# The u projection as a stage of its own behind q, k and v, read back from DRAM 512 tokens at a time

## The chip, the core and the metric

One NeuronCore of a Trainium2 chip runs the whole kernel in one launch. The metric is the device time of that launch in microseconds (us). Its engines are called PE (TensorE, the matrix unit), DVE (VectorE), ACT (ScalarE), POOL (GpSimd) and SP (SyncE, which issues most DMAs here); each works through its own instructions in order.

## The reference

One encoder block: 16 meta tokens ahead of 2048 tokens, 1024 wide, float32. Attention has 4 query heads and 2 key/value heads of 128; the second half of the block, u, is 512 wide and is mixed by a two-dimensional Fourier transform over tokens and over each group's 128 channels.

```python
hn = rms_norm(h, g_mix)
proj = hn @ w_in                      # q 512, k 256, v 256, u 512
q = axial_rope(rms_norm(q, g_q)); k = axial_rope(rms_norm(k, g_k))
attn = softmax(q @ k.T / sqrt(128)) @ v
f = fft2(u as 4 groups of 128, axes=(tokens, channel), norm="ortho").real
four = f @ w_fourier                  # by group
mixed = concat(rms_norm(attn, g_attn_out), rms_norm(four, g_fourier_out))
h = h + mixed @ w_out
h = h + relu(rms_norm(h, g_mlp) @ w_up)**2 @ w_down
return rms_norm(h, g_final)[:, 16:]
```

## The kernel before

A float32 operand is split into a high and a low part (cast by ACT, remainder by DVE's L71), and a product is three matmuls: high x high, low x high, high x low (mm3, lines L80, L81, L82; L83 to L85 in the changed file). Where the text says "split", it means this. Both halves of a split are needed before the low matmuls can run.

The stages follow one another in the program, and within most of them two generators are interleaved by hand:

- *Chunks j = 0 to 7 of 256 tokens.* `prep` loads x (`load_x`, on SP), normalizes it, transposes it on PE (pt) and splits it into hth and htl. `proj_qkv` multiplies by the weights of q (tile pq) and of k and v (pkv), 512 columns at a time, for two halves of 128 tokens. `proj_u` multiplies the same parts by the weights of u, 256 tokens at a time, and adds the result (pu) into two resident tiles, UA and EV, which hold sums and differences of mirrored tokens. `post` norms and rotates q and k, splits q, k, v, transposes (ptq, ptk) and stores them to DRAM (q_d, k_d, v_d); it is a generator that `side()` advances between the projections. The meta rows' k and v (pkv_m, t = 16) come behind chunk 7.
- *Folds.* `fold` and `fold_even` (lines L506 to L517) halve UA and EV once more on DVE and ACT. They stand in chunk 7, between `proj_u` and `proj_qkv`.
- *Fourier.* `fourier`: channel products pa from EV and UA (with rem, a few rows put together on DVE), split into ahi and alo; then products py with table tiles thi, tlo, 258 columns wide; results go back into EV, UA through DVE.
- *Attention*, generator `attention`, in 16 units. A unit has 18 steps and lags 2 steps over the next (UNIT = 20). A step makes two score tiles (s, three matmuls each), copies them to S on ACT, and keeps running maxima M on DVE. When M is complete, PE transposes it (pm_m), and the maxima mb come from that. Then DVE subtracts mb from S, ACT takes the exponential, DVE adds to acc, splits the weights into ph and pl, and PE multiplies them by v (o). S_BUFS = 8 tiles of scores are kept. Units 0 and 1 (`NATIVE = 2`) don't split: PE multiplies the float32 S by vn directly (L842).
- *out_f* (pof: the Fourier half through w_fourier and w_out), then *poa* and the *MLP* (pup, pdn) and last block-wise products (ux, uy, dx, dy).

`att.upto(n)` runs attention up to step n; `mix(gen, n, a0, a1)` spreads steps a0 to a1 over the n yields of another stage. Before, Fourier takes steps 0 to 30 (FLEAD), out_f most of 30 to 84, its last five yields (HELD) 84 to 88, the MLP the rest. The pools give the buffers, the framework the waits; each engine's order is the program's with little moved.

Of the kernel before, what the change touches and what calls it, by code (L numbers as in the profile page):

```python
# [40 lines left out]
NATIVE = 2  # L41
# [6 lines left out]
FLEAD = 30  # L48
SKIP = 5
# [86 lines left out]
def encoder_block(ctx: ExitStack, tc: tile.TileContext, x, meta, w_in, w_f,  # L136
# [18 lines left out]
    mid = Lines(tc.alloc_tile_pool(name="mid", bufs=1), small)  # L155
    edge = ctx.enter_context(tc.tile_pool(name="edge", bufs=1, side="right"))
# [3 lines left out]
    wu = Lines(tc.alloc_tile_pool(name="wu", bufs=1, side="right"), small)  # L160
# [39 lines left out]
    h_d = [dram.tile([P, D], F32, name=f"h_d{t}") for t in range(NT)]  # L200
    m_d = dram.tile([P, KT, 512], F32, name="m_d")
# [72 lines left out]
    def prep(j):  # L274
# [10 lines left out]
        for kk in range(KT // 2):  # L285
# [27 lines left out]

    def spread_m():

        shape = [P, 2, MR // META, META]
        hT["m"] = []
        for kq in range(KT // 4):
            tiles = [t2k(f"ht{e}_m_{kq}", [P, 4, MR]) for e in "hl"]
            for i in range(2):  # L320
                for t, src, eng in zip(tiles, hT[LAST][2 * kq + i], (nc.scalar.copy, nc.vector.tensor_copy)):
                    eng(t[:, 2 * i:2 * i + 2].rearrange("p k (r n) -> p k r n", n=META),
                        bc(f32v(src[:, :, 256:]).rearrange("p k (r n) -> p k r n", r=1), shape))
            hT["m"].append(tiles)
# [5 lines left out]

    def proj_u(j):
        n = 256 + META if j == LAST else 256
        n0 = META + 256 * j
        for cp in range(0, NG, 2):
            if j == LAST:
                pss = [bank(f"pu_{j}_{cp + c}", (P, 1, n)) for c in range(2)]
            else:
                pss = [(tbank if j == 0 and cp == 0 else bank)(f"pu_{j}_{cp}", (P, 2, n))]
            for c in range(2):
                cc = 1024 + (cp + c) * P  # L340
                o = pss[c][:, 0] if j == LAST else pss[0][:, c]
# [47 lines left out]
    def post(j, a, pq, pkv):  # L389
# [14 lines left out]
        with ExitStack() as behind:  # L404
            for i in first_acts if m else ():
                behind.enter_context(tc.issue_after(i))
            for h in range(h0, 6):
                nc.scalar.activation(t1[:rows, h], src(h), AF.Square, accum_out=ss[:rows, h:h + 1])
# [30 lines left out]
        for _ in range(4 if j == 0 else 1):  # L439
            yield  # L440
# [61 lines left out]
    def fold(src, g):  # L502

        t = tp.tile([P, D], F32, name=f"fold{g}", tag="x", bufs=3)[:, :QUART]
        low, high = src[:, g, 0:QUART], src[:, g, QUART + 1:HALF + 1][:, ::-1]
        nc.vector.tensor_tensor(t, low, high, op=ALU.add)  # L506
        nc.vector.tensor_tensor(high, low, high, op=ALU.subtract)
        nc.scalar.copy(low, t)
# [1279 lines left out]
```

## Time and profile before

| | |
|---|---|
| median of 3 runs (lowest, highest) | 2293.54 us (2292.48, 2294.43) |
| span of the profiled execution | 2291.4 us |
| PE busy | 2278.1 us, 99% |
| DVE busy | 1718.7 us, 75% |
| ACT busy | 1280.6 us, 56% |
| POOL busy | 184.0 us, 8% |
| DMA | 307.23 MB, mean 134 GB/s |

The profiled execution's own time is its span. Matmuls overlap in PE's pipeline, so a PE that is shown busy is not necessarily at its peak: a 512-wide matmul is recorded with 0.39 us, while the next starts 0.23 us behind it.

Rough places in the trace: chunks up to 304 us, the meta rows' pkv_m to 309.4, pa from 309.9, py 315.0 to 417.3, scores from 327.2, pof from 424.5, poa from 587.5, pup from 623.1, ux from 1674.2.

### The profile page before, as it was taken

Reading aid. Unit: us, or ns where it says so; the run is one execution under the profiler, and the core shown is the slowest. Engines: PE = TensorE matmul, PEld = TensorE weight load, DVE = VectorE, ACT = ScalarE, POOL = GpSimd, SP = SyncE. Lnnn points to the kernel's source line nnn. Section 1 sums busy time; section 2 is a strip of 40 time slices with the busy share of each in tenths; the row PEclk is TensorE's granted clock in tenths of the full one; section 3 lists DMA queues with packets and bytes.
Section 4 is the critical chain, followed back from the end, with each engine's and each line's share of the span. In section 5 each row is a group of like instructions: output and inputs, shape, how many; then the busy total and the mean of one; then the engine's idle time right before and its main releaser. Section 6 shows DMA issues by size and latency. Waiting matters only on the chain.

```text
span 2291.4 us, 30005 instructions
## 1 busy us (share of the span) xinstructions
PE 2278.1 (99%) x10846; PEld 1883.0 (82%) x10846; DVE 1718.7 (75%) x2448; ACT 1280.6 (56%) x2303; POOL 184.0 (8%) x235
## 2 busy tenths in 40 slices
PE   9999999999999999999999999999999999999998
PEld 7888988777888888888888888888888888888887
DVE  6435588999986877986887877885875656697796
ACT  6443356566665655665765775664665545543344
POOL 2212120222000000000000100000000000200000
PEclk9999999999999999999999999999999999999999
DMA  6343252543533222333342453224454444865442
GB/s 213 100 119 102 78 169 79 190 137 120 166 117 108 96 87 79 114 114 106 97 157 87 157 175 104 92 82 170 140 177 158 152 152 156 303 193 165 129 138 83
DMA packets 178069, 307.23 MB, mean 134 GB/s; under 512 B 14960, under 2 KB 63728, under 8 KB 177536
## 3 DMA queue, kind: packets, MB, share of 16 engines
q1 hardware_dynamic: 159136, 262.89, 34.9%
q0 software_dynamic: 18640, 42.16, 6.2%
q8 instruction: 85, 1.39, 0.3%
q14 instruction: 64, 0.52, 0.1%
q10 hardware_dynamic: 144, 0.26, 0.0%
HBM read 225.27 MB, written 79.99 MB: 133 GB/s over the span
## 4 chain that ended last, share of the span: by engine, by line
PE 94%; DVE 3%; DMA 1%; ACT 1%; issue 1%; POOL 0%; SPq 0%; POOLq 0%; DVEq 0%; ACTq 0%
PE pdn L80 5%; PE pdn L82 5%; PE pdn L81 5%; PE pup L80 5%; PE pup L82 5%; PE pup L81 5%; PE s L80 3%; PE s L82 3%; PE s L81 3%; PE ux L80 2%; PE ux L81 2%; PE ux L82 2%; PE dx L80 2%; PE dx L82 2%; PE dx L81 2%; PE o L81 2%
## 5 line engine op out<-in xcount | busy, mean ns | idle before, releaser
L80 PE MATMUL pdn<-wh_dn,ah 128*128 128x512 f32 x512 | 201.5, 394 | 0.2 <-ACT r L1154 0.2
L80 PE MATMUL pup<-mTh,wh_up 128*128 128x512 f32 x512 | 201.5, 394 | 0.0
L81 PE MATMUL pup<-mTl,wh_up 128*128 128x512 f32 x512 | 200.7, 392 | 0.0
L82 PE MATMUL pup<-mTh,wl_up 128*128 128x512 f32 x512 | 200.4, 391 | 0.0
L81 PE MATMUL pdn<-wl_dn,ah 128*128 128x512 f32 x512 | 199.9, 390 | 0.0
L82 PE MATMUL pdn<-wh_dn,al 128*128 128x512 f32 x512 | 198.7, 391 | 0.0
L773 ACT COPY S<-s 128x512 f32<-128x512 f32 x256 | 148.4, 584 | 55.6 <-PE s L82 48.5
L70 ACT CAST wh_up<-wr_up 128x512 fp32r<-128x512 f32 x128 | 79.4, 620 | 164.3 <-PE pup L81 76.5
L832 DVE TENSOR_TENSOR S<-S,mb 128x1024 f32<-128x1024 f32 x128 | 154.8, 1218 | 8.4 <-ACT mb L803 8.2
L71 DVE TENSOR_TENSOR pl<-S,ph 128x512 fp32r<-128x512 f32 x196 | 132.3, 696 | 11.0 <-ACT ph L70 10.7
L833 ACT ACTIVATE S<-S 128x1024 f32<-128x1024 f32 x114 | 120.7, 1060 | 34.7 <-DVE S L832 34.1
L70 ACT CAST wh_dn<-wr_dn 128x512 fp32r<-128x512 f32 x128 | 79.1, 620 | 107.9 <-PE pdn L82 52.6
L71 DVE TENSOR_TENSOR wl_up<-wr_up,wh_up 128x512 fp32r<-128x512 f32 x128 | 87.6, 687 | 68.1 <-ACT wh_up L70 63.3
L839 DVE TENSOR_TENSOR acc<-acc,S 128x1024 f32<-128x1024 f32 x110 | 134.1, 1219 | 1.3 <-ACT S L833 1.1
L71 DVE TENSOR_TENSOR wl_dn<-wr_dn,wh_dn 128x512 fp32r<-128x512 f32 x128 | 87.2, 687 | 60.2 <-ACT wh_dn L70 51.8
L70 ACT CAST ph<-S 128x512 fp32r<-128x512 f32 x196 | 118.7, 620 | 15.9 <-PE o L82 12.5
L70 ACT CAST ah<-a 128x1024 fp32r<-128x1024 f32 x56 | 58.5, 1048 | 118.2 <-issue 60.8
L779 DVE TENSOR_TENSOR M<-M,S 128x1024 f32<-128x1024 f32 x96 | 118.0, 1229 | 6.7 <-ACT S L773 6.0
L80 PEld LDWEIGHTS pdn<-wh_dn,ah 128*128 128x128 f32 x512 | 96.1, 188 | 23.5 <-ACT r L1154 3.6
L80 PE MATMUL s<-q,kt 128*128 128x512 f32 (+1 forms) x272 | 113.0, 415 | 0.1
L82 PEld LDWEIGHTS pdn<-wh_dn,al 128*128 128x128 f32 x512 | 96.2, 188 | 19.9
L82 PEld LDWEIGHTS pup<-mTh,wl_up 128*128 128x128 f32 x512 | 96.2, 188 | 19.4
(345 smaller groups left out, 6413.0 us busy)
## 6 DMA issues: line engine op xcount, KB each, us to landing
wr_up<-in_w_up_dram SPq DMA_DIRECT2D x128, 256.0 KB, 2.8
wr_dn<-in_w_down_dram SPq DMA_DIRECT2D x128, 256.0 KB, 2.6
a<-s_d SPq DMA_DIRECT2D x42, 512.0 KB, 3.6
R<-in_w_up_dram SPq DMA_DIRECT2D x16, 1024.0 KB, 5.2
s_d<-s SPq DMA_DIRECT2D x64, 256.0 KB, 2.2
d<-in_w_down_dram SPq DMA_DIRECT2D x26, 512.0 KB, 5.0
s_d<-c SPq DMA_DIRECT2D x48, 256.0 KB, 2.4
x<-in_x_dram SPq DMA_DIRECT2D x16, 512.0 KB, 4.9
```

The lines of the kernel that those rows point to most:

```text
L70: self.high = nc.scalar.copy(hi, src)
L71: self.low = nc.vector.tensor_tensor(lo, src, f32v(hi), op=ALU.subtract)
L80: nc.tensor.matmul(out, a[0], b[0], start=first, stop=False, skip_group_check=chain)
L81: nc.tensor.matmul(out, a[0], b[1], start=False, stop=False, skip_group_check=chain)
L82: nc.tensor.matmul(out, a[1], b[0], start=False, stop=last, skip_group_check=chain)
L773: nc.scalar.copy(S[:, i % 2], ps)
L779: nc.vector.tensor_tensor(M, M, S, op=ALU.max)
L832: nc.vector.tensor_tensor(S, S, mb, op=ALU.subtract)
L833: nc.scalar.activation(p, S, AF.Exp, scale=ISQ)
L839: nc.vector.tensor_tensor(acc, acc, p, op=ALU.add)
```

## The change

- `proj_u` goes. In each chunk, `prep` also stores hth and htl to u_d in DRAM (64 stores of 256 KB on SP's queue). u_d has four blocks of 512 tokens.
- The weights of u are loaded and split in chunks 2 to 5 (two k per chunk), instead of at the start.
- Behind pkv_m comes `u_stage`: four parts of four result tiles each (pu_0 to pu_3), 8 values of k per part, matmuls 512 tokens wide. Parts 0 and 1 each cover one block of tokens and all 4 groups of channels; parts 2 and 3 each cover two blocks and two groups. It reads u_d back, 512 KB per load (hu), one load per k in parts 0 and 1 and two in parts 2 and 3, into 6 buffers (HG_BUFS), and yields after each k. The folds of parts 2 and 3 are queued as `todo`: one per yield while there are matmuls, and the rest in yields of their own behind the last matmul.
- The 16 meta tokens' u has matmuls of its own (`u_meta`: pum, pumt); before they rode on chunk 7's matmuls, which were 272 wide for that.
- The first 4 yields of u_stage (U_FIRST) come before attention starts; the others take attention steps 0 to 62 (ULEAD). Fourier then takes 62 to 84, out_f 84 to 104 (ALEAD = 20), the step to the MLP 4 more; the MLP starts at 108 instead of 88.
- `NATIVE = 0`: units 0 and 1 are split like the others.
- Unit 0's scores use the same two PSUM buffers as the others' instead of alternating with a free bank.

```diff
-NATIVE = 2
+NATIVE = 0
 LAG = 2
 WAKE = 6
 UNIT = 18 + LAG
 TURNS = 3
 LEAD = 4
 AHEAD = 30
-FLEAD = 30
-SKIP = 5
+ULEAD = 62
+FLEAD = 84
+U_FIRST = 4
+ALEAD = 20
+HG_BUFS = 6
...
+            for e, t in enumerate((hi, lo)):
+                nc.sync.dma_start(u_d[j // 2][:, 2 * kk:2 * kk + 2, e, j % 2 * 256:j % 2 * 256 + 256], f32v(t))
...
-    def proj_u(j):
...
-            for _ in proj_u(0):
-                side()
...
-                for src in (EV, UA):
-                    for g in range(NG):
-                        fold(src, g)
-                    for g in range(0, NG, 2):
-                        fold_even(src, g)
-                wu.release()
-                ft = Lines(tc.alloc_tile_pool(name="ft", bufs=1, reuse_waits="tile"), small)
-                load_tables(0)
+            if 2 <= j < 6:
+                for k in (2 * j - 4, 2 * j - 3):
+                    load_w(k, 1024)
+                    split_w(k, 1024)
...
+    def u_stage():
+
+        todo = []
+        for n, part in enumerate(([(0, g) for g in range(NG)], [(1, g) for g in range(NG)],
+                                  [(b, g) for b in (2, 3) for g in (0, 1)], [(b, g) for b in (2, 3) for g in (2, 3)])):
+            ps = {bg: bank(f"pu_{n}_{i}") for i, bg in enumerate(part)}
+            for k in range(KT):
+                h = {}
+                for b in sorted({b for b, _ in part}):
+                    h[b] = hg.tile([P, 2, 512], R32, name=f"hu_{n}_{b}_{k}", tag="hu", bufs=HG_BUFS)
+                    nc.sync.dma_start(f32v(h[b]), u_d[b][:, k])
+                for b, g in part:
+                    mm3(nc, ps[b, g], w_op(k, 1024 + g * P, 1024 + (g + 1) * P), (h[b][:, 0], h[b][:, 1]),
+                        k == 0, k == KT - 1, True)
+                    if k == KT - 1:
+                        n0 = META + 512 * b
+                        y = ps[b, g]
+                        if b < 2:
+                            nc.scalar.copy(UA[:, g, n0:n0 + 512], y)
+                        else:
+                            r = slice(L - n0 - 511, L - n0 + 1)
+                            y = y[:, ::-1]
+                            nc.vector.tensor_tensor(EV[:, g, r], UA[:, g, r], y, op=ALU.add)
+                            nc.vector.tensor_tensor(UA[:, g, r], UA[:, g, r], y, op=ALU.subtract)
+                if todo:
+                    f, *of = todo.pop(0)
+                    f(*of)
+                yield
+            if n == 1:
+                nc.vector.tensor_tensor(EV[:, :, 1025:1032], UA[:, :, 1025:1032], UA[:, :, 1033:1040][:, :, ::-1], op=ALU.add)
+                nc.vector.tensor_tensor(UA[:, :, 1025:1032], UA[:, :, 1025:1032], UA[:, :, 1033:1040][:, :, ::-1],
+                                        op=ALU.subtract)
+                nc.vector.tensor_copy(EV[:, :, 1032:1033], UA[:, :, 1032:1033])
+            if n > 1:
+                g = part[0][1]
+                todo += [(fold, src, i) for src in (EV, UA) for i in (g, g + 1)]
+                todo += [(fold_even, src, g) for src in (EV, UA)]
+        for f, *of in todo:
+            f(*of)
+            yield
+
+    us = u_stage()
+    for i in range(U_FIRST):
+        side()
+        if i == 1:
+            u_meta()
+        next(us)
+    drain(*pend)
...
-            if u == 0 and i % 2:
-                ps = bank("s_" + nm)
-            else:
-                ps = app.tile([P, 512], F32, name="s_" + nm, tag="S", bufs=2)
+            ps = app.tile([P, 512], F32, name="s_" + nm, tag="S", bufs=2)
...
+    mix(us, 38 - U_FIRST, 0, ULEAD)
+    hg.release()
+    wu.release()
+    ft = Lines(tc.alloc_tile_pool(name="ft", bufs=1, reuse_waits="tile"), small)
+    load_tables(0)
+    fp = Lines(tc.alloc_tile_pool(name="fp", bufs=1, reuse_waits="tile"), small)
+    four = fourier()
...
-    mix(with_weights(four, 9), 19, 0, FLEAD, SKIP - 1)
+    mix(with_weights(four, 10), 20, ULEAD, FLEAD)
...
-    mix(itertools.islice(of, 34 - HELD), 34 - HELD, FLEAD, need[0])
-    mix(of, HELD, need[0], need[0] + LEAD)
+    mix(itertools.islice(of, 34 - HELD), 34 - HELD, FLEAD, need[0] + ALEAD)
+    mix(of, HELD, need[0] + ALEAD, need[0] + ALEAD + LEAD)
```

How each engine's order changes at three places. The names are those of the text above with the numbers of chunk, unit, part or buffer behind them.

**DVE, the folds.** Before, in chunk 7, as pu of the last groups comes in:

```order
L362 TENSOR_TENSOR EV_70<-UA_69,pu_7_2_3000 128x256
L363 TENSOR_TENSOR UA_69<-UA_69,pu_7_2_3000 128x256
L506 TENSOR_TENSOR fold2_3078<-EV_70 128x516
L507 TENSOR_TENSOR EV_70<-EV_70 128x516
L357 COPY UA_69<-pu_7_3_3001 128x16
L358 COPY EV_70<-pu_7_3_3001 128x1
L533 MEMSET rem0_3122 128x384
L362 TENSOR_TENSOR EV_70<-UA_69,pu_7_3_3001 128x256
```

At that place PE goes on with chunk 7's pq and pkv, 96 matmuls of 512 columns behind the last one of pu_7_3:

```order
L82 MATMUL pu_7_3_3001<-hth_7_3_2843,wl512_7_326 128x272
L80 MATMUL pq_7_0_3147<-wh1024_0_212,hth_7_0_2641 128x512
L81 MATMUL pq_7_0_3147<-wl1024_0_213,hth_7_0_2641 128x512
L82 MATMUL pq_7_0_3147<-wh1024_0_212,htl_7_0_2642 128x512
L80 MATMUL pq_7_0_3147<-wh1024_1_218,hth_7_0_2641 128x512
L81 MATMUL pq_7_0_3147<-wl1024_1_219,hth_7_0_2641 128x512
```

Now DVE has, behind the last pu of part 3 (EV and UA <- pu), the same folds among the softmax of units 2 and 3:

```order
L74 TENSOR_TENSOR pl_2_7_0_3983<-S_2_6_3497,ph_2_7_0_3982 128x512
L74 TENSOR_TENSOR pl_2_7_1_3990<-S_2_6_3497,ph_2_7_1_3989 128x512
L787 TENSOR_TENSOR M_3_3947<-M_3_3947,S_3_4_3979 128x1024
L471 TENSOR_TENSOR fold2_4002<-EV_70 128x516
L471 TENSOR_TENSOR fold3_4014<-EV_70 128x516
L472 TENSOR_TENSOR EV_70<-EV_70 128x516 x2
L847 TENSOR_TENSOR acc_2_3835<-acc_2_3835,S_2_8_3558 128x1024
L74 TENSOR_TENSOR pl_2_9_0_4020<-S_2_8_3558,ph_2_9_0_4019 128x512
L74 TENSOR_TENSOR pl_2_9_1_4027<-S_2_8_3558,ph_2_9_1_4026 128x512
L787 TENSOR_TENSOR M_3_3947<-M_3_3947,S_3_6_4012 128x1024
L840 TENSOR_TENSOR S_2_10_3611<-S_2_10_3611,mb_2_3788 128x1024
L471 TENSOR_TENSOR fold2_4047<-UA_69 128x516
```

The folds moved from beside the projections of chunk 7 to between steps of M, acc and pl of attention.

**PE, behind the last matmul of u.** Now, from the last pu_3_3 to the first pa:

```order
L85 MATMUL pu_3_3_3637<-hu_3_3_7_3951,wl512_7_1663 128x512
L83 MATMUL s_3_4_3975<-q_3_3839,kt_0_1_1_3326 128x512
L84 MATMUL s_3_4_3975<-q_3_3839,kt_0_1_1_3326 128x512
L85 MATMUL s_3_4_3975<-q_3_3839,kt_0_1_1_3326 128x512
L83 MATMUL o_2_3836<-ph_2_7_0_3982,vt_0_1_1_3334 128x512
L83 MATMUL s_3_5_3996<-q_3_3839,kt_0_1_1_3326 128x512
L84 MATMUL s_3_5_3996<-q_3_3839,kt_0_1_1_3326 128x512
L85 MATMUL s_3_5_3996<-q_3_3839,kt_0_1_1_3326 128x512
L83 MATMUL s_3_6_4008<-q_3_3839,kt_0_1_1_3326 128x512
L84 MATMUL s_3_6_4008<-q_3_3839,kt_0_1_1_3326 128x512
L85 MATMUL s_3_6_4008<-q_3_3839,kt_0_1_1_3326 128x512
L535 MATMUL pa0_0_4207<-cw0_298,EV_70 128x128
```

Where pq and pkv followed the last u before, there are now scores of unit 3 and value products of unit 2, and then pa, the first Fourier products.

**SP, chunk 0.** Before, behind the fourth pair of weights (wraw0 and wraw512 are the q, k, v weights of one k):

```order
L226 DMA wraw512_3_155<-in_w_in_dram 128x512
L483 DMA gqk_140<-g_rows 128x512
L170 DMA x_1_0_277<-in_x_dram 128x1024
L170 DMA x_1_1_279<-in_x_dram 128x1024
L226 DMA wraw0_4_236<-in_w_in_dram 128x512
```

Now, from the last of the eight stores of chunk 0's parts:

```order
L300 DMA u_d0_130<-htl_0_3_220 128x2x256
L230 DMA wraw0_4_249<-in_w_in_dram 128x512
L230 DMA wraw512_4_251<-in_w_in_dram 128x512
L230 DMA wraw0_5_259<-in_w_in_dram 128x512
L230 DMA wraw512_5_261<-in_w_in_dram 128x512
L230 DMA wraw0_6_269<-in_w_in_dram 128x512
L230 DMA wraw512_6_271<-in_w_in_dram 128x512
L230 DMA wraw0_7_279<-in_w_in_dram 128x512
L230 DMA wraw512_7_281<-in_w_in_dram 128x512
L451 DMA gqk_144<-g_rows 128x512
L173 DMA x_1_0_290<-in_x_dram 128x1024
L173 DMA x_1_1_292<-in_x_dram 128x1024
```

x_1, the tokens of chunk 1, moved behind eight stores of u_d and the weights of k = 4 to 7.

More of the change, by code (lines that the diff above doesn't have):

```diff
@@ L155, in encoder_block @@
     mid = Lines(tc.alloc_tile_pool(name="mid", bufs=1), small)
+    wu = Lines(tc.alloc_tile_pool(name="wu", bufs=1), small)
     edge = ctx.enter_context(tc.tile_pool(name="edge", bufs=1, side="right"))
@@ L200, in encoder_block @@
     h_d = [dram.tile([P, D], F32, name=f"h_d{t}") for t in range(NT)]
+    u_d = [dram.tile([P, KT, 2, 512], F32, name=f"u_d{b}") for b in range(4)]
     m_d = dram.tile([P, KT, 512], F32, name="m_d")
@@ L319, in spread_m @@
             tiles = [t2k(f"ht{e}_m_{kq}", [P, 4, MR]) for e in "hl"]
[L320 to L323, printed above, removed]
+            for e, (t, eng) in enumerate(zip(tiles, (nc.scalar.copy, nc.vector.tensor_copy))):
+                eng(t.rearrange("p k (r n) -> p k r n", n=META),
+                    bc(f32v(hm[:, 4 * kq:4 * kq + 4, e]).rearrange("p k (r n) -> p k r n", r=1), shape))
             hT["m"].append(tiles)
@@ L403, in post @@
         src = lambda h: pq[:rows, h * P:(h + 1) * P] if h < 4 else pkv[:rows, (h - 4) * P:(h - 3) * P]
[L404 to L408, printed above, removed]
+        for h in range(h0, 6):
+            nc.scalar.activation(t1[:rows, h], src(h), AF.Square, accum_out=ss[:rows, h:h + 1])
         rs = rstd_of(tp, ss[:rows, h0:], 6 - h0, HD, f"h{h0}", rows)
@@ L632, in encoder_block @@
                     a += 1
-            if j != LAST:
-                for _ in proj_u(j):
-                    side()
         for _ in nxt:
@@ L641, in encoder_block, with u_meta @@
     wqk.release()
-    fp = Lines(tc.alloc_tile_pool(name="fp", bufs=1, reuse_waits="tile"), small)
+    hg = Lines(tc.alloc_tile_pool(name="hg", bufs=1, reuse_waits="tile"), small)
+    def u_meta():
+        ps = bank("pum")
+        for k in range(KT):
+            nc.tensor.matmul(ps[:2 * META], hm[:, k].rearrange("p l n -> p (l n)"), W[k, 512][0], start=k == 0, stop=False,
+                             skip_group_check=True)
+            nc.tensor.matmul(ps[:META], hm[:, k, 0], W[k, 512][1], start=False, stop=k == KT - 1, skip_group_check=True)
+        um = hg.tile([P, 512], F32, name="um")
+        nc.scalar.copy(um[:2 * META], ps[:2 * META])
+        both = hg.tile([P, 64], F32, name="both")
+        nc.vector.tensor_tensor(both[:2 * META, :META], ident[:2 * META, :META], ident[:2 * META, META:2 * META], op=ALU.add)
+        pt = bank("pumt", (P, NG, META))
+        for g in range(NG):
+            nc.tensor.matmul(pt[:, g], um[:2 * META, g * P:(g + 1) * P], both[:2 * META, :META], start=True, stop=True)
+        nc.vector.tensor_copy(UA[:, :, 0:META], pt)
+        nc.vector.tensor_copy(EV[:, :, 0:1], pt[:, :, 0:1])
@@ new lines, in u_stage @@
+    def u_stage():
[3 more added lines that the diff above has]
+            ps = {bg: bank(f"pu_{n}_{i}") for i, bg in enumerate(part)}
+            for k in range(KT):
+                h = {}
[30 more added lines that the diff above has]
+            f(*of)
+            yield
@@ L684, in fourier @@
                 yield
-    four = fourier()
-    next(four)
-    drain(*pend)
-    trp.release()
-    tp.release()
     app = tc.alloc_tile_pool(name="app", bufs=1, space=PSUM)
@@ L896, in attention @@
             yield
-    HELD = 5
+    HELD = 0
     wt = {}
@@ L1239, in encoder_block @@
     n0, n1 = 8 + 2 + 8 * 15 + 8, 8 + 8 * 13 + 8 + 4
-    a0, a2 = need[0] + LEAD, need[3] + 1
+    a0, a2 = need[0] + ALEAD + LEAD, need[3] + 1
     a1 = a0 + (a2 - a0) * n0 // (n0 + n1)
```

80 lines of the change are left out of this document (19 added, 61 removed).

## The prediction

> **What bounds the kernel now.** I read the page first, then a table of stages cut at the starts of pm_m, then PE's waits, and last single instructions for prices. In the page's first part the figures are busy time, share of the span and instructions. In the second each digit is a fortieth of the span.
>
> ```profile
> span 2291.4 us, 30005 instructions
> PE 2278.1 (99%) x10846; PEld 1883.0 (82%) x10846; DVE 1718.7 (75%) x2448; ACT 1280.6 (56%) x2303; POOL 184.0 (8%) x235
> PEclk9999999999999999999999999999999999999999
> GB/s 213 100 119 102 78 169 79 190 137 120 166 117 108 96 87 79 114 114 106 97 157 87 157 175 104 92 82 170 140 177 158 152 152 156 303 193 165 129 138 83
> PE 94%; DVE 3%; DMA 1%; ACT 1%; issue 1%; POOL 0%; SPq 0%; POOLq 0%; DVEq 0%; ACTq 0%
> ```
>
> TensorE is the bound and its clock is full throughout: what the change takes from PE's work is worth its full time, and every us for which PE stands still is lost. But the average hides one region. VectorE stands at 75% over the span, but not evenly.
>
> The next table gives each stretch, its length, then busy time by engine. It is cut where PE computes the row maxima of attention units 0 to 5 (pm_m; each waits for the unit's last M on DVE).
>
> ```profile
> 342.80:394.40 51.60, 51.60 (x308) 41.57 (x309) 46.50 (x65) 33.49 (x57) 3.57 (x5) 1.00 0.29 78
> 394.40:450.50 56.10, 55.45 (x274) 42.02 (x271) 53.94 (x78) 32.19 (x58) 15.93 (x19) 1.00 0.53 169
> 450.50:510.30 59.80, 58.82 (x267) 46.80 (x267) 57.60 (x82) 37.55 (x75) 13.60 (x17) 1.00 0.41 143
> 510.30:568.40 58.10, 58.02 (x261) 45.50 (x260) 56.05 (x77) 36.06 (x67) 13.06 (x19) 1.00 0.37 123
> 568.40:653.90 85.50, 85.50 (x405) 70.20 (x406) 69.65 (x106) 52.85 (x95) 7.54 (x8) 1.00 0.47 149
> 653.90:741.30 87.40, 87.40 (x393) 71.86 (x392) 69.40 (x93) 53.51 (x88) 4.13 (x6) 1.00 0.39 118
> ```
>
> In the second to fourth stretch DVE is busy 96% of the time, beside a PE that is at its limit too: both engines carry the same load there. From the fifth on DVE has slack. So the question to the change is not only what PE saves, but where it leaves DVE's work without PE work beside it.
>
> **Prices.** A busy PE row overlaps the next one, so prices are steps from start to start.
>
> ```profile
> 73.97 0.28 PE L81 MATMUL pu<-htl,wh 128*128 128x256 f32 x1
> 76.61 0.28 PE L82 MATMUL pu<-hth,wl 128*128 128x256 f32 x1
> ...
> 76.95 0.60 PE L291 MATMUL pt<-ident,x 128*128 128x128 f32 x4
> 77.30 0.36 PE L80 MATMUL pu<-hth,wh 128*128 128x256 f32 x1
> ...
> 100.06 0.39 PE L80 MATMUL pq<-wh,hth 128*128 128x512 f32 x1
> 103.24 0.39 PE L82 MATMUL pq<-wh,htl 128*128 128x512 f32 x1
> ...
> 369.63 1.88 PE L842 MATMUL o<-S,vn 128*128 128x512 f32 x4
> 370.94 0.79 PE L80 MATMUL s<-q,kt 128*128 128x512 f32 x1
> 371.58 0.40 PE L81 MATMUL s<-q,kt 128*128 128x512 f32 x1
> ```
>
> 73.97 to 76.61 are 22 steps of 256 columns: 0.120 us. Four of 128 columns take 0.35 (76.95 to 77.30), so I put the small ones (pa, pm, pd) at 0.1. 100.06 to 103.24 are 14 steps of 512: 0.227. From 369.63 to 371.58 run four records of the unsplit value product and one split one: (1.95 - 0.23) / 4 = 0.43 each.
>
> ```profile
> L80 PE MATMUL pu<-hth,wh x256: 277/283/365, 33.0 to 281.0; 128*128 128x256 f32 x112, 128*128 128x272 f32 x16
> L842 PE MATMUL o<-S,vn x64: 590/592/697, 347.9 to 440.5; 128*128 128x512 f32 x64
> ...
> 519.35 0.69 DVE L71 TENSOR_TENSOR ohl<-O,ohl 128x512 fp32r<-128x512 f32 x1
> 519.96 0.42 DVE L71 TENSOR_TENSOR yl<-UA,yh 128x256 fp32r<-128x256 f32 x1
> 520.29 1.22 DVE L839 TENSOR_TENSOR acc<-acc,S 128x1024 f32<-128x1024 f32 x1
> 521.43 0.42 DVE L873 TENSOR_TENSOR sq<-sq,O 128x256 f32<-128x256 f32 x1
> 521.76 0.74 DVE L957 SCALAR_TENSOR_TENSOR xo<-pof,rs_f,xo 128x512 f32<-128x512 f32 x1
> 522.42 0.66 DVE L873 TENSOR_TENSOR sq<-sq,O 128x256 f32<-128x256 f32 x1
> ```
>
> DVE's steps: 512 elements 0.61, 256 elements 0.33, 1024 elements 1.14, a scalar-tensor-tensor of 512 0.66. Over many such pairs the medians are 0.605, 0.335 and 1.137, which I use.
>
> **PE's work: -7.3 us.** Each of the three lines of a split product has 256 matmuls of pu, 768 in all: 768 x 0.120 = 92.2, against 384 x 0.227 = 87.2 of twice the width, -5.0. The value products of units 0 and 1: 64 x 0.43 = 27.5 against 96 x 0.227 = 21.8, -5.7. The meta tokens' own projection adds 16 matmuls of 512 and four small ones, less 16 columns on the last chunk's 256: +3.4.
>
> [...]
>
> **Chunks: +4 us (0 to 8).** In chunk 0 the u matmuls (33.0 us on) fill the time until the next tokens' transposes and the first post. They are gone, and on SP's queue eight stores of chunk 0's parts and eight weight loads now stand ahead of x_1.
>
> ```profile
> 12.00:20.00 8.00, 8.00 (x37) 6.64 (x36) 7.95 (x14) 7.39 (x16) 1.09 (x1) 1.00 0.94 333
> 20.00:40.00 20.00, 20.00 (x118) 17.74 (x117) 14.99 (x27) 14.60 (x37) 5.35 (x5) 1.00 0.58 189
> x<-in_x_dram SPq DMA_DIRECT2D x16, 512.0 KB, 4.9
> kt<-k_d POOLq DMA_DIRECT2D x15, 512.0 KB, 4.2
> ```
>
> The DMA engines are 94% busy from 12 to 20 us. 2 MB of stores at 333 GB/s are 6 us; with 4.9 us to land, x_1 comes at about 28 us, and its norm, transposes and DVE's post of chunk 0 then lie open. I take 4, between hidden and the 6 us plus a round of the post. The later stores (2 MB per chunk of some 26 us: 81 GB/s, beside rates up to 303 elsewhere) I cost at nothing; what hides them is that nobody reads u_d until the stage behind. Weights of u, loaded in chunks 2 to 5, likewise.
>
> **Into the u stage: +0.7 us (-3 to +5).** Behind the last pkv the first part needs hu loads. The second hu load stands on SP behind v_m's store, which waits for DVE's post of the meta rows; 4 to 5 us of landing follow. I expect 5 us of stall there plus some 1.5 on ptk. It takes the place of nearly as much: PE's instructions up to pm_m of unit 0 at 342.8 come to 327.7 us by the prices above, 15.1 are lost, and 5.9 of these lie behind the last pkv, at the first Fourier products and scores.
>
> **Units 3 and 4: +27 us (20 to 38).** This is the term that decides. After the last pu matmul, PE has only attention of units 2 and 3 and the small pa until the first py: 76 x 0.227 and 24 x 0.1 for pa and pm, 19.6 us. In DVE's order the same stretch holds the last pu's eight additions, the folds, rem, tables, alo, and the split softmax of two units: 13 instructions of 1024, 43 of 512, a few small ones, 41.5 us. Before, the folds stood beside the last chunk's 512-wide projections:
>
> ```profile
> L506 DVE TENSOR_TENSOR fold<-EV x4: 691/691/692, 273.6 to 282.9; 128x516 f32<-128x516 f32 x4
> ```
>
> Counted from pm_m of unit 2 to that of unit 3, DVE now has 22 x 1.137 + 46 x 0.605 + small = 54.7 us of instructions and PE 154 x 0.227 + small = 38.1. From unit 3 to unit 4 (most of the Fourier products): DVE 22 x 1.137 + 60 x 0.605 + 4 x 0.66 + 34 x 0.335 + small = 78.6; PE 320 x 0.12 + 94 x 0.227 + small = 67.7. Both are instruction streams in order, so pm_m can't come before DVE's sum: at full rate 16.6 + 10.9 = 27.5 us of standing PE. Counted in the same way, before has DVE 52.8 and 52.4, PE 56.0 and 54.8, for the 59.8 and 58.1 of the third and fourth row: 7.1 us of waiting.
>
> DVE doesn't reach the full rate: 44.0 us of instructions take 46.5 of busy time in the first row (POOL 3.6) and 52.8 take 57.6 in the third (POOL 13.6). The POOL work that goes with it belongs to out_f, which now comes later, so I take the nearer first row, 0.95: 57.6 + 82.7, a stall of 34.5, less 7.1: +27.4. At full rate +20.4; at the third row's whole length (0.88), 62 + 89, +38.
>
> **Elsewhere: -6.1 us.** By the same count, unit 1 waits 5.4 us before (51.6 for 46.2 of PE's work); with DVE 39.1 beside PE 53.0 I leave it 1.2. Unit 2 pays 3.3 instead of 2.4, unit 5 1.5 instead of 2.3: -4.1. The MLP's units get 217 steps of attention instead of 237 beside them; before, ten of them lose 11.5 us, of which I take 2 back. The hu loads, 25 MB over some 150 us of mixed work, I cost at nothing: six buffers are three steps of 4.9 us ahead of 4 to 5 us of landing.
>
> **Sum.** -7.3 + 4 + 0.7 + 27.4 - 6.1 = +18.7 on the profiled 2291.4, 2310.1. The median of the runs, 2293.54, lies 2.1 above the profiled span, so 2312.
>
> **Rivals.** *Faster: DVE works ahead.* In units 1 and 2 the changed order has PE 109.9 against DVE 90.8. If DVE used these 19.1 us for rows that now stand behind, the stall would fall to 27.5 - 19.1 = 8.4, the term to +1.3, the sum to -7.4: 2286. For it speak the eight score buffers (S_BUFS); against it that M and pl read PE's and ACT's output of the same unit, so DVE can be only a few rows ahead. It decides from a stall below 11 us in units 3 and 4. *Partly:* full rate, nothing lost in the chunks, and a third of that slack: about +1, 2295. *Worse: the hu loads are late.* If PE waits 1 us in each of the 16 steps of the parts that need two loads, +16: 2328. Against it: 214 GB/s would do, and the page has slices at 303. [...]
>
> **Chances.** The forecast (2302 to 2322) 0.52; DVE ahead 0.18; partly 0.14, most of it within 0.2%; hu late 0.11; clock 0.05. 0.2% is 4.6 us, about what a measurement of this kernel can tell from no change. That gives faster 0.19, same 0.10, slower 0.71. The range 2285 to 2327 leaves out half of "DVE ahead" and most of "hu late".
>
> **What would show it.** Right: in the profile after, waits of PE for pl, M, ahi and py's parts between the last pu and pm_m of unit 4, some 30 us in all, with DVE over 90% busy there; pm_m of units 2 to 3 57 us apart and 3 to 4 83; 4 us of waits at 33 to 41 us and 5 us at the first hu. Wrong: DVE below 90% there or the two distances near 40 and 70; or the waits are on DMA. If PE's steps of pu at 512 are above 0.227, the first term is mis-sized.

## The result, and the profile after

The changed kernel takes 2345.2 us (median of four runs, 2344.18 to 2350.03) against 2293.09 beside it: a ratio of 1.0233, 95% interval 1.0218 to 1.0247. It is 52 us slower. The forecast had the direction, +18.7 us, and its range ended at 2327.

The page of the changed kernel, the same lines as shown of before:

```profile
span 2342.4 us, 29610 instructions
PE 2289.1 (98%) x10518; PEld 1875.6 (80%) x10518; DVE 1737.9 (74%) x2463; ACT 1298.6 (55%) x2331; POOL 186.0 (8%) x235
PE 77%; DVE 1%; DMA 1%; ACT 1%; issue 0%; POOLq 0%; POOL 0%; DVEq 0%; ACTq 0%
```

PE's busy time has grown by 11.0 us. Its work by the steps from start to start has fallen (ledger below), so the growth is PE shown busy below its peak. The table of stretches, cut at pm_m of units 0 to 6, shows those of units 1, 2, 3, 4 and 6; a unit's stretch runs from pm_m of the unit before it to its own. The columns are length, then busy time of PE, PE's weight loads, DVE, ACT, POOL, each with its number of instructions, then the granted clock (1.00 is full speed), the DMA share and GB/s:

```profile
283.20:338.00 54.80, 54.76 (x246) 42.84 (x246) 40.52 (x47) 33.03 (x54) 3.58 (x5) 1.00 0.43 127
338.00:395.50 57.50, 57.50 (x260) 47.18 (x261) 53.29 (x72) 32.65 (x53) 4.13 (x6) 1.00 0.84 270
395.50:453.80 58.30, 47.60 (x203) 35.06 (x202) 56.78 (x82) 37.74 (x62) 0.71 (x1) 0.93 0.24 80
453.80:535.40 81.60, 79.16 (x559) 72.55 (x557) 79.31 (x137) 52.86 (x99) 0.72 (x1) 0.99 0.23 67
651.50:735.70 84.20, 80.92 (x374) 65.75 (x373) 67.73 (x102) 56.02 (x100) 5.45 (x7) 0.98 0.42 136
```

The third line is the stretch of unit 3: DVE busy 97% of it, PE 82%, and the clock at 0.93. PE's waits now name what was not there before:

```profile
PE pt L295 <- ACT x L254: 12.1, 6, 2.9
PE pu L83 <- DMA hu<-u_d: 11.1, 2, 8.3
PE s L83 <- DMA q<-q_d: 5.8, 2, 3.1
PE o L84 <- DVE pl L74: 4.1, 3, 1.9
PE o L83 <- ACT ph L73: 2.9, 3, 1.7
```

The columns are us in total, times, longest. DVE's share of the waiting (pl, the fourth line) is not the largest: the transposes of x in the chunks and the loads of hu are.

For a ledger of all 2342 us I gave every PE record its price by width, as in the prediction but by records (512 columns 0.227, 256 and 258 0.120, 128 or fewer 0.109, a record of an unsplit 512-wide product 0.43), and called lost what its step to the next record's start takes beyond the price. It leaves 22.6 us lost in the kernel before and 80.3 in the changed one:

| stretch | forecast | lost before | lost after | measured |
|---|---|---|---|---|
| PE's work | -7.3 | | | -6.6 (2260.4 to 2253.8) |
| chunks, first pq to last pkv | +4 | 1.8 | 21.4 | +19.6 |
| from there to pm_m of unit 0 | +0.7 | 1.6 | 15.9 | +14.3 |
| units 3 and 4 | +27.4 | 5.1 | 24.1 | +19.0 |
| units 1, 2 and 5 | -4.1 | 3.2 | 2.4 | -0.8 |
| unit 6 | in "elsewhere" | 0.3 | 6.4 | +6.1 |
| all others | -2 | 10.6 | 10.1 | -0.5 |

Where the chunks lose it: at 79.3, 106.5, 136.3 and 163.8 us PE's step to the first transposes of a chunk takes 2.5 to 3.4 us (idle for 2.0 to 2.9 of it). The second of them on ACT's timeline and on PE's (start, duration, engine, operation, and in brackets the idle time before it with its releaser):

```profile
103.86 1.15 ACT L254 ACTIVATE x<-x,rs_x 128x1024 f32<-128x1024 f32 x1 [0.93 <-POOL rs_x L195]
106.24 0.72 ACT L76 ACTIVATE wh<-wraw,cols 128x512 fp32r<-128x512 f32 x1 [1.23 <-DMA wraw<-in_w_in_dram]
106.87 0.58 ACT L249 ACTIVATE jk<-x 128x512 f32<-128x512 f32 x1
...
108.75 1.15 ACT L254 ACTIVATE x<-x,rs_x 128x1024 f32<-128x1024 f32 x1 [0.56 <-POOL rs_x L195]
```

```profile
109.95 0.55 PE L295 MATMUL pt<-ident,x 128*128 128x128 f32 x3 [2.92 <-ACT x L254]
```

ACT's cast of u's weights (wh) stands between the two halves of the norm of x and waits for its load; the last half of the norm (jk, then x) stands behind it, and PE behind that.

Where the entry loses it: SP issues the first hu at 237.00 and the second only 8 us later, behind v_m's store.

```profile
237.00 0.60 SPq L621 DMA_DIRECT2D hu<-u_d  x1
...
243.54 1.31 SPq L402 DMA_DIRECT2D v_m<-vt  x1
244.95 0.57 SPq L621 DMA_DIRECT2D hu<-u_d  x1
```

```profile
240.99 0.77 PE L83 MATMUL pu<-hu,wh 128*128 128x512 f32 x1 [2.75 <-DMA hu<-u_d]
241.56 0.63 PE L84 MATMUL pu<-hu,wh 128*128 128x512 f32 x1
...
244.97 0.39 PE L85 MATMUL pu<-hu,wl 128*128 128x512 f32 x1
245.20 0.33 PE L421 MATMUL ptk<-ident,qn 96*128 96x96 f32 x2
253.86 0.80 PE L83 MATMUL pu<-hu,wh 128*128 128x512 f32 x1 [8.34 <-DMA hu<-u_d]
254.45 0.63 PE L84 MATMUL pu<-hu,wh 128*128 128x512 f32 x1
```

The second hu took 8.9 us from issue to use (median 5.1 for all). Behind both waits the matmuls are recorded with 0.63 instead of 0.39 us and follow one another after 0.43 instead of 0.23, about half the rate. The table of stretches, for the 4 us from the wait's end and the next 4, shows the clock at half in its clock column, and then back (0.52, then 1.00):

```profile
253.80:257.70 3.90, 3.84 (x9) 3.10 (x10) 0.00 (x0) 0.00 (x0) 2.84 (x4) 0.52 1.03 420
257.70:261.70 4.00, 4.00 (x19) 3.23 (x19) 0.00 (x0) 0.00 (x0) 2.01 (x4) 1.00 1.16 408
```

Steps at half speed add up to 8.6 us of the 80.3.

### The profile page after: what moved, and what is told of

It reads as the page before. It is cut to its first block, busy times and chain, and to the rows that moved or that the text cites. A ratio compares the mean times of both kernels' runs of the same rounds, so it can differ in the third digit from the quotient of the medians.

```text
span 2342.4 us, 29610 instructions
## 1 busy us (share of the span) xinstructions
PE 2289.1 (98%) x10518; PEld 1875.6 (80%) x10518; DVE 1737.9 (74%) x2463; ACT 1298.6 (55%) x2331; POOL 186.0 (8%) x235
## 4 chain that ended last, share of the span: by engine, by line
PE 77%; DVE 1%; DMA 1%; ACT 1%; issue 0%; POOLq 0%; POOL 0%; DVEq 0%; ACTq 0%
PE pdn L83 5%; PE pdn L85 5%; PE pdn L84 5%; PE pup L84 5%; PE pup L85 5%; PE pup L83 5%; PE ux L83 2%; PE ux L84 2%; PE ux L85 2%; PE dx L85 2%; PE dx L84 2%; PE dx L83 2%; PE s L83 2%; PE o L83 2%; PE o L85 2%; PE o L84 2%
## 5 line engine op out<-in xcount | busy, mean ns | idle before, releaser
L84 PE MATMUL pup<-mTl,wh_up 128*128 128x512 f32 x512 | 200.2, 391 | 0.0
L74 DVE TENSOR_TENSOR pl<-S,ph 128x512 fp32r<-128x512 f32 x224 | 151.0, 695 | 16.6 <-ACT ph L73 16.2
L73 ACT CAST ph<-S 128x512 fp32r<-128x512 f32 x224 | 135.9, 620 | 29.6 <-PE o L85 24.9
L787 DVE TENSOR_TENSOR M<-M,S 128x1024 f32<-128x1024 f32 x96 | 117.3, 1222 | 10.1 <-ACT S L781 9.6
```

Of the source, the lines that this page charges most:

```text
L73: self.high = nc.scalar.copy(hi, src)
L74: self.low = nc.vector.tensor_tensor(lo, src, f32v(hi), op=ALU.subtract)
L84: nc.tensor.matmul(out, a[0], b[1], start=False, stop=False, skip_group_check=chain)
L787: nc.vector.tensor_tensor(M, M, S, op=ALU.max)
```

## The experiments

Each experiment is the changed kernel with the edit shown, except two that start from the kernel before and say so. Lost time is by the ledger, from one profile each. The totals have intervals of about 0.15% each way, so an edit worth 5 us does not show clear of them alone; the stretch that it touches does. One scatter has to be known: the chunks, where the edit leaves them alone, took 224.0 to 229.7 us in seven kernels and lost 20 to 26, with half-speed matmuls in most.

**1. The weights' splits at the end of the chunk.**

```diff
             if 2 <= j < 6:
                 for k in (2 * j - 4, 2 * j - 3):
                     load_w(k, 1024)
-                    split_w(k, 1024)
...
+            if 2 <= j < 6:
+                for k in (2 * j - 4, 2 * j - 3):
+                    split_w(k, 1024)
```

> The changed kernel, with one edit: the splits of u's weights (wh512, wl512) stand at the end of chunks 2 to 5 instead of their start; the loads stay where they are. Theory A, ACT blocked in order: in the changed kernel PE waits 2.5, 3.4, 2.8 and 3.0 us at the starts of four chunks (79.3, 106.5, 136.3, 163.8 us) for the norm of x, because ACT's cast of wh512 stands ahead of the last half of that norm and waits for a weight load that is queued behind the stores of u_d. Then these four waits go, and with them the half-speed matmuls behind the second: 11 to 14 us faster than the changed kernel's 2345, about 2333. Rival B, the x loads themselves come late because they stand on SP behind the stores and the DMA engines are 75% busy: the four waits stay, 0 to 2 us.

2339.65 us, ratio 1.021 (1.0194 to 1.0225). The four waits at the chunks' starts are gone, the longest there is 1.3; the chunks take 218.4 us and lose 14.5 instead of 21.4, none at half speed.

```profile
PE pt L295 <- ACT x L254: 6.8, 6, 1.3
PE pu L83 <- DMA hu<-u_d: 13.3, 2, 10.2
```

So ACT's order is the cause of that part, 6.9 us (1.6 of it the half-speed steps behind the second wait), and not 11 to 14: what remains at five chunk starts is a wait that costs 1.2 to 1.3 us and that the longer one had covered. Of the 14.5 us, 4.9 stand in chunk 0, 6.4 at these five starts, 0.9 at the meta tokens' transposes, and 2.3 in smaller pieces. The wait for hu grew by 2 us; the total gains 5.6.

**2. The first six hu loads together, ahead of the meta rows' post.**

```diff
+        for k in range(HG_BUFS):
+            first[k] = hg.tile([P, 2, 512], R32, name=f"hu_0_0_{k}", tag="hu", bufs=HG_BUFS)
+            nc.sync.dma_start(f32v(first[k]), u_d[0][:, k])
+        yield
...
     us = u_stage()
+    next(us)
```

> The changed kernel, with one edit: the first six hu loads of the u stage are issued on SP together before the meta rows' post (kt_15, v_m, kt_16), instead of one by one between its parts. Theory A, order on SP: the second hu was issued 7.9 us behind the first (244.95 against 237.00), beside the attention loads of kt (1.8 MB on POOL's queue), and took 8.9 us to land; ahead of them it lands before PE needs it. PE's wait of 8.3 us goes and so do the half-speed matmuls behind it: 9 to 12 us faster than the changed kernel, about 2335; the first wait of about 3 us stays. Rival B, bandwidth: the same 3 MB of hu and 1.8 MB of kt have to come at 391 GB/s anyway, the six loads share it, the first hu now lands later: gain below 4 us.

2340.92 us, ratio 1.0213 (1.0196 to 1.023).

```profile
PE pu L83 <- DMA hu<-u_d: 4.6, 3, 2.9
```

The long wait is gone, and time lost from the last pkv to pm_m of unit 0 falls from 15.9 to 9.9 us. pm_m of unit 1 stands at 330.9 instead of 338.0. Theory A holds for the place, and the first wait of some 3 us stays, as it said; of the gain, about half of what was expected came: 5.7 us between the last pkv and pm_m of unit 1, 4.3 between the medians. The DMA engines are fully busy here (share 1.01, 328 GB/s over the 44 us), so that waits of 0.5 to 1.2 us on later loads take the long one's place: part of rival B is true.

**3. Fewer attention steps beside Fourier.**

```diff
-FLEAD = 84
+FLEAD = 70
```

> The changed kernel, with one number: Fourier takes attention steps 62 to 70 instead of 62 to 84, out_f 70 to 104 instead of 84 to 104. Theory A, DVE bounds unit 4's stretch (81.6 us from pm_m of unit 3 to that of unit 4, where PE has 67.7 us of work by the prices of the prediction): now the same stretch has PE 102.0 against DVE 94.7, so its 13.9 us of PE's waiting go, 10 to 15 us faster, about 2332. Rival B, the Fourier chain itself (pa, alo, py, and back) sets the pace and not DVE's total: 0 to 4 us.

2345.26 us, ratio 1.0227 (1.0211 to 1.0242): nothing. Units 4 and 5 together take 195.8 us instead of 197.7 and lose 5.1 instead of 6.9.

```profile
455.70:571.30 115.60, 113.91 (x723) 101.91 (x722) 103.26 (x180) 68.84 (x142) 23.14 (x24) 0.99 0.45 142
571.30:651.60 80.30, 80.30 (x371) 66.11 (x370) 65.20 (x97) 40.42 (x78) 38.96 (x31) 1.00 0.53 180
```

There was little to win, because PE's work in unit 4's stretch is not 67.7 us. The trace has 128 records of pa there, where the program has 64 matmuls: these are unsplit float32 products with two records each, 14.2 us and not 6.4. By records the stretch has 75.6 us of work in 81.6. Neither theory: the price was wrong.

**4. Without the last part's folds.**

```diff
-                todo += [(fold, src, i) for src in (EV, UA) for i in (g, g + 1)]
-                todo += [(fold_even, src, g) for src in (EV, UA)]
+                if n == 2:
+                    todo += [(fold, src, i) for src in (EV, UA) for i in (g, g + 1)]
+                    todo += [(fold_even, src, g) for src in (EV, UA)]
+                else:
+                    todo += [(int,)] * 6
```

> The changed kernel without the folds of the last part of the u stage (groups 2 and 3 stay unfolded, so the Fourier products read other data): twelve DVE instructions of 512 elements, 7.3 us, and their ACT copies are left out; the attention steps beside them stay. Theory A, DVE bounds unit 3's stretch (58.3 us against 38.1 of PE's work): 6 to 8 us faster, about 2338. Rival B, the stretch is set by the chain of the attention steps (scores, copy, maxima, exponential, split), with DVE's folds in its gaps: 0 to 3 us.

2344.26 us, ratio 1.0228 (1.0212 to 1.0243). Unit 3's stretch takes 51.1 us instead of 58.3, the 7.2 that theory A has. Unit 4's takes 85.5 instead of 81.6, and the chunks, with code unchanged, 228.4 instead of 225.4; so the total shows nothing. Of the 7.2 us, 3.9 come back in the next stretch; 3.3 are left over the two, hardly more than rival B's 3.

**5. Unit 2 without the split.** A second way to take DVE's work out of the same stretch.

```diff
-            native = u < NATIVE
+            native = u == 2
```

> The changed kernel, but unit 2 multiplies by v without a split, as units 0 and 1 did before: 16 DVE splits of 512 elements (9.7 us) and 16 ACT casts leave the stretch from pm_m of unit 2 to that of unit 3, and PE gets some 3 us more work there (32 records of 0.43 in place of 48 of 0.227). Theory A, DVE's total bounds this stretch (58.3 us, PE's work by its records 40.2): it falls to 48 to 50 us, the kernel 8 to 10 us faster, about 2336. Rival B, the chain of steps bounds it: 58 to 61 us, no gain or 3 us slower.

2339.87 us, ratio 1.0205 (1.019 to 1.022).

```profile
400.20:448.80 48.60, 45.14 (x187) 31.57 (x186) 46.97 (x66) 29.09 (x46) 4.13 (x6) 0.98 0.46 140
```

Unit 3's stretch falls by 9.7 us to 48.6, lost time from 18.1 to 5.6, with 2.9 us more of PE's work. DVE's total bounds this stretch: shown by two edits with the sizes expected. (A step of 3.2 us at 448.4 in the changed kernel, with a wait for q of the next unit, stands in it too, and this edit keeps one of 2.9; DVE is busy for all but 1.5 us of the 58.3, so that wait sets little of the length.) Here nothing comes back (unit 4 takes 81.7). The total is 5.3 us down, since the chunks of this kernel took 3.9 more.

**6. Out_f's last yields kept for the unmixed steps.**

```diff
-    HELD = 0
+    HELD = 5
```

> The changed kernel with the last five yields of out_f kept for the four attention steps before the MLP, as before the change (HELD = 5 instead of 0). Theory A: at 652 us PE waits 3.1 us for q of the next unit, which has one buffer and is loaded only behind the last score of the unit before, and some matmuls behind it run at half speed, because these four steps have no other PE work beside them; with pof beside them the load is covered and the unit's 6.4 us of lost time fall to 1 or 2: 4 to 5 us faster, about 2340.5. Rival B: the cover is missed where the yields were taken from, nothing gained, within 1.5 us.

2342.12 us, ratio 1.0199 to 1.0233 around 1.0216. Units 5 and 6 take 102.5 and 93.4 us, 195.9 together instead of 200.2; unit 6 loses 1.5 instead of 6.4, no clock below 1.00:

```profile
642.20:735.60 93.40, 93.40 (x438) 75.98 (x437) 72.72 (x111) 57.57 (x102) 8.26 (x11) 1.00 0.52 163
```

Theory A holds: with other PE work beside it, q's single buffer no longer shows as a wait of PE at this place.

**7. The kernel before, with units 0 and 1 split.** One part of the change alone.

```diff
-NATIVE = 2
+NATIVE = 0
```

> The kernel before, with one part of the change alone: units 0 and 1 are split too. PE saves 5.7 us of work, DVE gets 32 splits of 512 (19.4 us) and ACT 32 casts. Theory A, DVE is at its limit from 394 to 568 us (96% busy): unit 1's stretch takes about 54 us instead of 51.6, unit 2's about 65 instead of 56.1, unit 3's 62 instead of 59.8; the kernel is 8 to 14 us slower, about 2304. Rival B, PE is the bound there: 3 to 6 us faster.

2312.45 us, ratio 1.0091 (1.0075 to 1.0106): 19.7 us slower.

```profile
345.60:399.60 54.00, 50.28 (x318) 43.86 (x317) 52.47 (x75) 40.78 (x71) 3.58 (x5) 0.99 0.26 73
399.60:470.90 71.30, 61.81 (x318) 51.48 (x317) 64.54 (x95) 42.03 (x77) 24.15 (x19) 0.94 0.44 134
```

Units 1 and 2 take 54.0 and 71.3 us instead of 51.6 and 56.1, and unit 3 59.6 where 62 was expected. PE's work fell by 5.7, its lost time rose by 24.2, 2.6 of it at half speed in unit 2. Unit 1 came out as theory A had it. Unit 2 is 6 us longer than it said, and there DVE is not the bound (busy 64.5 of 71.3 us): the two longest waits of PE in this stretch, at 426 and 463 us, are for POOL and for a load of q (the first row below holds two shorter waits for q as well).

```profile
PE s L80 <- DMA q<-q_d: 7.9, 3, 4.5
PE pys L934 <- POOL ysq L929: 4.4, 1, 4.4
```

So splitting these two units cost 20 us here, but only a part of it through DVE's total.

**8. The changed kernel, with units 0 and 1 unsplit again.**

```diff
-NATIVE = 0
+NATIVE = 2
```

> The changed kernel with one part undone: units 0 and 1 multiply by v without a split again (NATIVE = 2). Theory A: beside u, their stretches have DVE 39 and 52 us against PE 54 and 57 and lose only 1.5 us, so PE's 5.7 us of extra work count in full: 5 to 6 us slower, about 2351. Rival B: DVE's and ACT's relief is worth as much as in the kernel before, where the split of these two units alone cost 20 us: 5 us faster or more.

2358.77 us, ratio 1.0282 (1.0267 to 1.0298): 13.6 slower. In units 1 and 2 (57.7 and 60.7 instead of 54.8 and 57.6) it is 6.0, as expected, all of it work. The profile has the rest in stretches whose code is the same: chunks 4.3 us longer (4.6 us of half-speed steps instead of 1.6), unit 4 1.3, the entry and unit 6 0.7 each. Why they lose more here was not tried.

**9. The norm of x one step earlier** (with edit 1, x in four buffers, and its loads at the start of `prep`).

```diff
-            for n, got in enumerate(proj_qkv(j)):
+            if j < LAST:
+                next(nxt)
+            for n, got in enumerate(proj_qkv(j)):
...
-            t = tp.tile([P, D], F32, name=f"x_{j}_{a}", tag="x", bufs=3)
+            t = tp.tile([P, D], F32, name=f"x_{j}_{a}", tag="x", bufs=4)
```

> The changed kernel with u's weights split at the end of the chunks (as in the run with that edit alone, which had 14.5 us of lost PE time in the chunks instead of 21.4), and besides the loads of x issued at the start of prep into four buffers, and the norm of the next chunk's x put one step earlier, ahead of the post's copy of v on ACT. Theory A, ACT's order: five waits of 1.3 us at the chunk starts (79, 106, 132, 159, 185 us) are what is left of the norm behind that copy; they go, 5 to 7 us faster than that run's 2339.7, about 2333.5. Rival B, they come from something else (buffers of PSUM, the stores): 0 to 2 us. Chunk 0's 5 us stay in both.

2345.51 us, ratio 1.023 (1.0214 to 1.0245): a miss for both, worse than edit 1 alone. The chunks lose 21.8 us again. The step also moved the norm's reader, the first transposes, which are the next step of the same generator; PE now waits there twice in a chunk (11 waits on x, 8.6 us). It says nothing about where the 1.3 us come from.

**10. The kernel before with short u products.**

```diff
-                for k in range(KT):
-                    mm3(nc, o, w_op(k, cc, cc + P), h_op(j, k, slice(0, n)), k == 0, k == KT - 1)
+                for k in range(1):
+                    mm3(nc, o, w_op(k, cc, cc + P), h_op(j, k, slice(0, n)), True, True)
```

> The kernel before with one of the eight k of u's products in the chunks, so u is incomplete: 672 matmuls of 256 columns, 80.6 us of PE's work, are left out of the chunks, and nothing is stored or moved. It asks where the 12 to 13 us of lost PE time in the changed kernel's chunks come from that don't go with the weights' edit. Theory A, u's matmuls were the cover of the norm of x and of the post: lost time in the chunks rises from 1.8 us to 10 or more though there are no stores; the kernel takes 2222 to 2230. Rival B, the stores of u_d and their queue are the cause: lost time stays below 5 us and the kernel takes 2213 to 2217.

2247.1 us, ratio 0.9805 (0.9789 to 0.9821): PE's work fell by 81.0, the time by 45.8. Theory A in direction, and far more than its 10 us: the chunks lose 32.8 us instead of 1.8, without any store of u_d:

```profile
11.20:259.40 248.20, 226.58 (x1102) 183.78 (x1100) 153.51 (x342) 131.12 (x413) 56.43 (x63) 0.97 0.45 132
```

```profile
PE pq L80 <- ACT hth L70: 5.7, 1, 5.7
PE ptq L444 <- DVE qn L422: 4.0, 6, 0.7
PE ptk L453 <- DVE qn L422: 3.3, 6, 0.6
```

u's matmuls were the cover of the post (qn), and in chunk 0 of the next tokens. The chunk 0 wait alone is 5.7 us. This kernel also has the folds in chunk 7, at which some 8 us of the loss stand (218 to 229 us). So it shows that u's matmuls hid waits in the chunks of the kernel before, and that they show without any stores; it does not size the changed kernel's loss, nor is it made of the same waits: there PE waits for x at the chunk starts, and for qn only 0.4 us.

**11. The changed kernel without most stores of u_d.**

```diff
-            for e, t in enumerate((hi, lo)):
+            for e, t in enumerate((hi, lo)) if j < 2 else ():
...
-                    nc.sync.dma_start(f32v(h[b]), u_d[b][:, k])
+                    nc.sync.dma_start(f32v(h[b]), u_d[0][:, k])
```

> The changed kernel without the stores of u_d in chunks 2 to 7 (48 of 64); the u stage reads the first block of tokens four times, so u is another. Theory A, lost cover: the chunks keep 14 to 18 us of lost PE time of their 21.4 (the weights' loads come sooner, so their part may go), the kernel takes 2338 to 2343. Rival B, the stores: lost time falls below 8 us, the kernel takes 2330 or less. The entry into the u stage reads as much as before: its 16 us stay in both.

2342.53 us, ratio 1.0217 (1.0201 to 1.0232).

```profile
11.20:230.90 219.70, 208.40 (x1007) 169.04 (x1005) 129.70 (x274) 116.70 (x386) 55.82 (x63) 1.00 0.54 164
```

The chunks lose 15.7 us, close to the 14.5 of edit 1: without stores ahead of them the weights come sooner. ACT's cast of them still waits 1.1 us for its load, but it runs at 101.8 us instead of at 106.2 in the same chunk, and no wait at a chunk start from 79 us on is above 1.3. So these stores cost through the queue that the weights share with them, and 14 to 16 us of loss do not come from the stores of chunks 2 to 7. The stores of chunks 0 and 1 were left in, so chunk 0's part is not tested here.

**12. Edits 1, 2, 5 and 6 together.**

> The changed kernel with four edits together: u's weights split at the chunks' end, the first six hu loads issued ahead, unit 2's value products unsplit, and out_f's last five yields kept for the four steps before the MLP (HELD = 5). If the gains seen apart add up (by their stretches 7 in the chunks, 6 to 7 up to pm_m of unit 1, 10 in unit 3, 4 to 5 in unit 6), the changed kernel's 2345.2 falls by 24 to 28 us, to 2317 to 2321, still 1% above the kernel before. Rival: what one edit wins the next stretch gives back, less than 15 us, above 2330.

2318.31 us, ratio 1.0111 (1.0095 to 1.0126): 26.9 us off the changed kernel, 25.4 over the kernel before. Lost time is 51.8 us instead of 80.3; by stretches 15.1 in the chunks, 10.8 up to pm_m of unit 0, and unit 3 back to 48.4 us:

```profile
11.00:230.10 219.10, 207.87 (x1007) 169.18 (x1006) 127.78 (x274) 116.58 (x386) 59.44 (x63) 1.00 0.72 222
384.10:432.50 48.40, 45.48 (x188) 31.79 (x187) 46.82 (x65) 29.13 (x46) 4.14 (x6) 0.96 0.46 141
```

The causes found apart add up. Of the 25.4 us that are left, 13 stand in the chunks and 9 between the last pkv and pm_m of unit 0; no edit here removes them. No version that computes the whole block beats the kernel before.

## Why the prediction was wrong

The direction was right, and so was the mechanism of the term that was to decide it. The size failed in two terms that were taken as small, the chunks and the entry into the u stage: 33.9 us together where 4.7 were forecast.

**PE's work** was right: -6.6 for -7.3, with the same price of 0.227 for a step of pu.

**The chunks** are the step that failed most, +19.6 for +4. Two parts of it fell. The weights of u, like the later stores, stood at nothing: the weights' loads stand on SP behind stores, ACT's casts stand ahead of a half of the norm, and that is 6 to 7 us with the clock's share (edits 1 and 11). And the cover of u was counted for chunk 0 only. There 4 us were about right: the pieces at 33 to 41 us come to 5. But u's matmuls stood in every chunk, and without them a wait at the next one's transposes shows at five more starts (1.2 to 1.3 us where nothing else is in the way), and pieces of some tenths elsewhere. Edit 10 shows that u's matmuls covered waits throughout the chunks of the kernel before. That the five waits in the changed kernel are of this kind is argued and not shown: what delays the norm there is open, since the one edit aimed at them (9) moved the reader too.

**Into the u stage**, +14.3 for +0.7. The place was right: hu behind v_m's store on SP. The size was off three times. The waits were 2.8 and 8.3 us rather than one of 5: the second load was under way together with 1.5 MB of kt, some stores and five more hu (DMA share 1.16 from 245.2 to 253.8 us, fully busy), and took 8.9 us instead of 4 to 5. Half-speed steps behind the two waits added 2.5. And the credit of 5.9 us "lost behind the last pkv" before was not there: the trace of before loses 1.6. Edit 2 shows the order on SP: issued ahead, the second hu still took 7.5 us to land, but PE's wait of 8.3 us for it had become one of 0.8.

**Units 3 and 4**, +19.0 for +27.4. The mechanism is shown for unit 3, and it is sized right there: 58.3 us for a forecast of 57.6, and edits 4 and 5 move it by 7.2 and 9.7 for the 7.3 and 9.7 us of DVE's instructions that they take. Unit 4's length is right too (81.6 for 82.7), and DVE is busy 97% of it, but no edit tests DVE as its bound. In the two 24.1 us were lost, where I had 34.5: PE had 2.1 us more work in unit 3 and 7.9 in unit 4 than I gave it, the latter from pa at 0.1 per written matmul, where the trace has two records of 0.109. And the kernel before lost 5.1 us there and not 7.1.

**Elsewhere**, -6.1 forecast, +4.8 measured. The same missing records made the kernel before look as if it lost 5.4 us in unit 1 and 15.1 before unit 0; it lost 0.5 and, from PE's first matmul to pm_m of unit 0, some 6. There was little waiting to win back. And unit 6, where five yields of out_f had stood beside four attention steps, was not looked at: HELD = 0 is a line of the diff, and I didn't ask what covered q's load there (edit 6).

**The rivals.** A lower clock had 0.05, a chance that rested on no run: in the kernel before it is 1.00 as long as PE has matmuls (to 2288 us). It came, on top of the forecast case: 8.6 us of half-speed steps, at one chunk start (106.5 us), the entry, unit 3 and unit 6. Behind the wait of 8.3 us the clock is 0.52 for 3.9 us, then 1.00; in unit 3 it fell although no step of PE in that stretch had been above 2.4 us, as shown below. "The hu loads are late" came true at the entry only, not in the parts with two loads, where no wait on hu appears. "DVE works ahead" did not happen: unit 3 stood at DVE's full sum.

## What to carry to other kernels

Work that is moved away leaves a hole where it had covered others: go through every place where it stood, not only the first, and ask what PE will wait for there. Before crediting a change with waits that it removes, check that the trace has them: count records, not written instructions, and see that price times count gives the stretch's length. Where a cast waits for a load, look at what stands behind it on its engine: here ACT's cast of wh, for products of u that began only at 240.99, waited 1.23 us for its load, and half of the norm of x came behind it, at 106.87, while PE stood for 2.92 us. And look at what a load stands behind on its queue: here the second hu was issued behind v_m's store, 7.9 us behind the first.

## What the runs showed of the hardware that I had not expected

The clock was halved without any single long stop. In unit 3's stretch of the changed kernel no step of PE up to 433.6 us is above 2.4 us, but between 429.0 and 433.6 PE is busy for 1.12 of 4.60 us, and the clock is at 0.50 for the 4.3 us behind:

```profile
424.00:429.00 5.00, 3.05 (x12) 1.91 (x11) 5.00 (x7) 2.09 (x5) 0.00 (x0) 1.00 0.01 2
429.00:433.60 4.60, 1.12 (x3) 0.71 (x4) 4.60 (x7) 2.70 (x4) 0.00 (x0) 0.79 0.00 0
433.60:437.90 4.30, 4.30 (x12) 3.28 (x10) 4.30 (x5) 3.74 (x6) 0.00 (x0) 0.50 0.01 2
```

The length of a stop alone did not decide it either. A step of 3.4 us at 106.5 was followed by a lower clock, and one of 3.0 at 163.8 was not; but one of 3.0 at 238.0, behind 1.3 us of small transposes, was:

```profile
106.00:114.00 8.00, 5.08 (x21) 3.93 (x19) 3.28 (x7) 5.62 (x19) 1.85 (x2) 0.80 0.71 213
163.80:172.00 8.20, 5.66 (x28) 4.54 (x27) 4.30 (x10) 4.97 (x19) 1.89 (x2) 1.00 0.68 205
237.80:241.00 3.20, 0.42 (x3) 0.24 (x3) 2.67 (x8) 1.94 (x8) 2.92 (x5) 0.92 0.76 235
241.00:244.00 3.00, 3.00 (x7) 2.42 (x8) 2.42 (x7) 0.77 (x2) 1.97 (x3) 0.51 1.06 284
```

So a wait on PE could cost more than itself: in this kernel six such places added 1.1 to 2.0 us of half-speed steps each. From change to change the granted clock is 0.50 or 0.51 in each of these six drops (for 3.4 us from 110.8, 240.5, 452.1 and 656.9, for 6.8 us from 250.8 and 431.7) and 0.99 or 1.00 between them. And the same code takes different times: the unedited chunks spread over 5.7 us between kernels (224.0 to 229.7), and the half-speed steps in them from none (edit 2, 20.1 us lost) to 4.6 us (edit 8, 25.8 lost). Whether the clock alone makes that spread was not tried.
